# Putting a factor's high and low part side by side in products of 512 columns, in the up products of a blocked MLP

## The chip, the core and the metric

The kernel runs on one NeuronCore of a Trainium2 chip. The metric is the device time of one execution in microseconds (us), lower is better. TensorE (PE in the profile, with its weight loads listed as PEld), VectorE (DVE), ScalarE (ACT) and GpSimd (POOL) each work through an instruction stream of their own in order and wait for each other by semaphores; SyncE (SP) starts transfers.

## The reference

A decoder trunk of two layers on one sequence of 512 tokens of width 1024: layer 0 mixes by multi-head latent attention, layer 1 by sliding-window attention, and each is followed by a layer norm, the MLP below and another layer norm. The change lies in the two MLPs.

```python
def _mlp(x, w_up, w_down):            # x (1, 512, 1024), w_up (1024, 4096), w_down (4096, 1024)
    h = jax.nn.relu(x @ w_up)
    return (h * h) @ w_down

for l in range(DEPTH):                # DEPTH = 2
    ...
    x = _layernorm(alpha * x + y, ln_mix_g[l], ln_mix_b[l])
    x = _layernorm(alpha * x + _mlp(x, mlp_w_up[l], mlp_w_down[l]), ln_mlp_g[l], ln_mlp_b[l])
```

## The kernel before

**Precision.** Every float32 operand is split in two float32r parts, a high one (ACT copies it, in `split`, L78) and a low one (DVE subtracts, L86). A product takes three matmuls in place of one: high weight by high factor, high weight by low factor, low weight by high factor. `three` lists them.

**Seven products.** The hidden layer is cut in four blocks (`Block(q)`, q = 0 to 3) of 1024 hidden features. Within a block the up projection and the down projection are each computed as seven products of quarter matrices, in the manner of Strassen and Winograd: up products U1, U2, U5, U3, U6, U7, U4 and down products D1 to D7. M5 below is what U5 leaves, and so on. An up product (`Block.up`) has two weight tiles (i = 0, 1), two column halves of each (j = 0, 1) and four contraction steps (k = 0 to 3). For each of these 16 places it issues the three matmuls of 256 columns, 48 in all, and accumulates the two halves j of a tile i side by side in one PSUM bank of 512 columns: two banks a product. Behind the first block the three matmuls of a step follow each other. In the first block (q = 0) the order is by passes: first all of high by high, then high by low, then low by high, so that the low parts are wanted two passes later than the high ones. A down product (`Block.down_`) is 24 matmuls of 512 columns, 12 for each of two token tiles t, in one bank each.

**What becomes of the up products** (`up_out`). U1 and U2 accumulate into the same pair of banks: ACT copies M1 out to a scratch tile `u` when U1 is done (L756), U2 adds itself onto it in the bank, and ACT takes the sum through a relu (L758). M5 and M3 stay in their banks until U6 is done. Then DVE forms u += M6 (L764), v = M5 - u (L765) and a11 = M3 + v (L767), and from v and u later a21 and a22 (L770, L773). The first product that needs a bank again waits until its last reader is done.

**Order.** Tables of steps set the order of the products, of both kinds and of neighbouring blocks: a prime marks the later block.

```python
SECOND_STEPS = "U'1 U'2 D5 D3 U'5 D6 D7 U'3 D4 U'6 U'7 U'4 D'1 D'2"
STEPS = "U'1 D5 U'2 D3 U'5 D6 D7 U'3 D4 U'6 U'7 U'4 D'1 D'2"
FIRST_STEPS, LAST_STEPS = "U'1 U'2 U'5 U'3 U'6 U'7 D'2 U'4 D'1", "U'1 D5 U'2 D3 U'5 D6 D7 U'3 U'6 U'7 U'4 D4"
```

FIRST_STEPS run block 0, SECOND_STEPS the ups of block 1 among the downs of block 0, STEPS those of block 2, LAST_STEPS those of block 3. PE's program is in the order in which it is written (`pe`). What DVE and ACT do is put in order by the compiler's scheduler, and then executed in that order.

**Supply.** A ring of four weight tiles (each with its high part `wh` and low part `wl`) runs ahead of PE: DMA, ACT's split, DVE's split, use. PSUM has eight banks: six rotate under the tag "mm", two ("tr") serve transposes and U6. The scratch tiles of the MLP are called `uv`, the factors of the down products `fac`. The x factors, a combination of quarters of x for each n, are in tiles "xt" (`XFactors.part`): before, high and low parts are in separate tiles, `xth` and `xtl`, each of which holds two n. L573 and L576 add what a down product has left in its bank onto the residual x and so free that bank.

Of the kernel before, what the change touches and what calls it, by code (L numbers as in the profile page):

```python
# [10 lines left out]
F32R = mybir.dt.float32r  # L11
AF = mybir.ActivationFunctionType
# [4 lines left out]
P = 128  # L17
# [16 lines left out]
BANDW = 384  # L34
POOL_O, POOL_SO = (0, 2), (0, 1, 2, 3)
WARM = 18

ON_POOL = ("w_h", "w_o", "w_sq", "w_so")

# [11 lines left out]
def build(tc, nc, io, out):  # L51
    with ExitStack() as top:
        cp = top.enter_context(tc.tile_pool(name="cp", bufs=1))
        wp = top.enter_context(tc.tile_pool(name="wp", bufs=1))
        xp = top.enter_context(tc.tile_pool(name="xp", bufs=1))
# [7 lines left out]
        def nm(s):  # L63
            n_names[0] += 1
            return f"{s}_{n_names[0]}"
# [32 lines left out]
        def pe(ins):  # L98
            tc.keep_in_program_order(ins)
# [255 lines left out]
        b = bank()  # L355
# [3 lines left out]
        both = [xp.tile([P, 4, S], F32, tag="xt", bufs=8, name=nm("xw")) for _ in range(4)]  # L359
        both = [z.rearrange("p a b -> p (a b)") for z in both]  # L360
# [108 lines left out]
        class TokMajor:  # L469
# [15 lines left out]
            def part(self, t, kp):  # L485
                while len(self.w) <= kp:
                    self.w.append(weights(self.name))
                if t not in self.b:
                    self.b[t] = bank()
                self.group(self.b[t], t, kp, self.w[kp])  # L490
                self.done.add((t, kp))
                if kp == 3:
                    self.evac(t, slice(0, 512), self.b[t])
# [149 lines left out]
        class XFactors(Factors):  # L643


            def __init__(self, mp):
                super().__init__(mp)
                self.tiles = {}
                self.xf = [None] * 2

            def part(self, n, p):
                at = {1: (0, 0), 2: (0, 1), 5: (1, 0), 3: (1, 1), 6: (2, 0), 7: (2, 1), 4: (3, p)}[n]
                tile = (at[0], p if n != 4 else 0)
                if tile not in self.tiles:
                    self.tiles[tile] = xp.tile([P, 2, 4, 256], F32R, tag="xt", bufs=8, name=nm(("xth", "xtl")[p]))
                return self.tiles[tile][:, at[1]]
# [34 lines left out]
        def mlp(src, gb, dst, mp):  # L691
# [12 lines left out]
            own_bank = {1: 1, 2: 1, 5: 5, 7: 7, 4: 7, 6: 6}  # L704
# [4 lines left out]
            class Block:  # L709
# [13 lines left out]
                def quarter(self, name):  # L723
                    if name not in self.g:
                        self.g[name] = mp.tile([P, 4, 256], F32, tag=name, bufs=1, name=nm(name))
                    return self.g[name]

                def up(self, n):
                    w = [weights("up") for _ in range(2)]
                    key = {3: 3}.get(n) or own_bank[n]  # L730
                    for i in range(2):
                        b = self.bank(("U", key), i)
                        wh, wl = w[i]
                        steps = list(product(range(3), range(2), range(4)))
                        if self.q:
                            steps.sort(key=lambda step: step[1:])
                        for p, j, k in steps:
                            c = slice(j * 512 + k * P, j * 512 + (k + 1) * P)
                            group(
                                b[:, j * 256 : j * 256 + 256],  # L740
                                three(wh[:, c], wl[:, c], src.part(n, 0)[:, k, :], src.part(n, 1)[:, k, :])[p : p + 1],
                                n not in (2, 4) and (p, j, k) == (0, 0, 0), (p, k) == (2, 3), skip_group_check=True,
                            )
                        self.up_out(n, i)
                        if (self.q, i) == (0, 0) and n in (1, 2):
                            with tc.high_priority():
                                src.turn(n + 1)

                def up_out(self, n, i):
                    pairs = slice(2 * i, 2 * i + 2)  # L750
                    of = lambda key: self.banks[("U", key), i].rearrange("p (a b) -> p a b", a=2)
                    done = None
                    if n == 1:
                        if i == 0:
                            self.u = self.down.scratch()
                        nc.scalar.activation(self.u[:, pairs], of(1), AF.Copy)  # L756
                    elif n == 2:
                        nc.scalar.activation(self.quarter("a12")[:, pairs], of(1), AF.Relu)  # L758
                        if i == 1:
                            nc.scalar.activation(self.g["a12"], self.g["a12"], AF.Square)  # L760
                    elif n == 6:
                        if i == 0:
                            self.v = self.down.scratch()
                        nc.vector.tensor_add(self.u[:, pairs], of(6), self.u[:, pairs])  # L764
                        nc.vector.tensor_sub(self.v[:, pairs], of(5), self.u[:, pairs])  # L765
                        done = "a11"
                        nc.vector.tensor_add(self.quarter(done)[:, pairs], of(3), self.v[:, pairs])  # L767
                    elif n == 7:
                        done = "a21"
                        nc.vector.tensor_sub(self.quarter(done)[:, pairs], self.v[:, pairs], of(7))  # L770
                    elif n == 4:
                        done = "a22"
                        nc.vector.tensor_add(self.quarter(done)[:, pairs], of(7), self.u[:, pairs])  # L773
                    if done and i == 1:
                        nc.scalar.activation(self.g[done], self.g[done], AF.Relu)
                        nc.scalar.activation(self.g[done], self.g[done], AF.Square)
# [49 lines left out]
            at = {}  # L826
# [20 lines left out]
            b = blocks[NFF - 1]  # L847
# [5 lines left out]
            class Hidden:  # L853
# [6 lines left out]
                def of(self, p, k, cols):  # L860
                    n = ((2, 1), (4, 0))[cols.start // 256][k // 4]
                    return b.fac[n][:, p, k % 4, cols.start % 256 : cols.start % 256 + P]
# [12 lines left out]
        with tc.tile_pool(name="mla", bufs=1) as mp:  # L875
# [62 lines left out]
            for kp in range(4):  # L938
                wh, wl = weights("w_kv")
# [123 lines left out]
            w = weights("w_uv")  # L1063
# [427 lines left out]
```

## Time and profile before

| | |
|---|---|
| three timed runs | 997.42, 997.08, 996.26 us, median 997.08 |
| the profiled execution | 996.2 us |
| its span in the trace | 994.1 us, so 2.1 us lie around it |
| PE busy | 984.1 us, 99% of the span |
| DVE busy | 767.5 us, 77% |
| ACT busy | 554.5 us, 56% |
| POOL busy | 247.0 us, 25% |
| chain that ended last | PE 97%, of which matmuls of line L110 89% |

Read it as follows. An engine's busy time is the time in which at least one of its instructions was executing; matmuls overlap at their ends, so a single one appears longer than the distance to the next. The chain that ended last is followed back from the last instruction: each piece of it is work that something later had to wait for. Times inside the trace count from the span's start. The MLP of layer 0 runs from about 172 to 500 us, that of layer 1 from about 653 to 981 us.

### The profile page before, as it was taken

The numbers are of one execution on the slowest core, as the hardware profiler recorded it, in microseconds if no ns is written. First come the engines' busy times: TensorE is split into PE (matmuls) and PEld (weight loads), VectorE is DVE, ScalarE is ACT, GpSimd is POOL, SyncE is SP. The second block draws the span as 40 slices with busy tenths as digits, with TensorE's granted clock in tenths as the row PEclk, the third lists the DMA queues.
The fourth block names the chain that finished last, engine by engine and source line by source line (L and its number), as shares of the span: only waits on it lengthen the run. The fifth ranks groups of instructions, "written<-read, shape, count | busy, mean of one in ns | idle before, by whom it ended". The sixth has DMA issues, their size and how long they took to land.

```text
span 994.1 us, 15912 instructions
## 1 busy us (share of the span) xinstructions
PE 984.1 (99%) x6136; PEld 889.6 (89%) x6136; DVE 767.5 (77%) x1240; ACT 554.5 (56%) x847; POOL 247.0 (25%) x267
## 2 busy tenths in 40 slices
PE   9999999999999999999999999999999999999996
PEld 9888888999899999998899988889998998999986
DVE  6589857988878769786684678688995986888746
ACT  5557644457547547646156688546663663764710
POOL 1242101312212212210025675332131122022002
PEclk9999999999999999999999999999999999999999
DMA  7431125399789977963323211439798798798332
GB/s 262 135 98 43 64 106 191 105 214 235 147 186 234 173 170 218 227 107 129 104 78 103 86 65 54 170 64 240 215 184 190 181 201 177 167 261 142 79 127 84
DMA packets 60246, 149.55 MB, mean 150 GB/s; under 512 B 5211, under 2 KB 9740, under 8 KB 60172
## 3 DMA queue, kind: packets, MB, share of 16 engines
q0 software_dynamic: 24320, 58.73, 33.1%
q1 hardware_dynamic: 35564, 89.49, 26.4%
q8 instruction: 48, 0.79, 0.3%
q10 hardware_dynamic: 288, 0.33, 0.1%
q14 instruction: 26, 0.21, 0.1%
HBM read 146.41 MB, written 4.22 MB: 152 GB/s over the span
## 4 chain that ended last, share of the span: by engine, by line
PE 97%; DVE 1%; issue 0%; DMA 0%; ACT 0%; POOLq 0%; POOL 0%; DVEq 0%
PE mm L110 89%; PE tr L110 5%; PE tr L1130 1%; PE tr L1313 1%; PE tr L668 1%; PE tr L1315 1%; DMA xw<-in_xT 0%; PE tr L454 0%; PE mm L1054 0%; PE tr L908 0%; POOLq L1487 0%; POOL rs L416 0%; ACT p L1293 0%; DVE mm L1109 0%; DVE ql L86 0%
## 5 line engine op out<-in xcount | busy, mean ns | idle before, releaser
L110 PE MATMUL mm<-wh,fac 128*128 128x512 f32 (+1 forms) x944 | 283.5, 386 | 0.0
L78 ACT ACTIVATE wh<-wq 128x1024 fp32r<-128x1024 f32 x164 | 173.5, 1060 | 190.0 <-PE mm L110 134.9
L86 DVE TENSOR_TENSOR wl<-wq,wh 128x1024 fp32r<-128x1024 f32 x164 | 199.2, 1220 | 69.5 <-ACT wh L78 68.9
L110 PE MATMUL mm<-xth,wh 128*128 128x256 f32 (+1 forms) x936 | 222.1, 290 | 0.0
L110 PE MATMUL mm<-xth,wl 128*128 128x256 f32 (+1 forms) x808 | 210.5, 290 | 0.0
L110 PEld LDWEIGHTS mm<-wh,fac 128*128 128x128 f32 x944 | 175.6, 188 | 35.1 <-DVE fac L86 0.6
L110 PE MATMUL mm<-xtl,wh 128*128 128x256 f32 (+1 forms) x680 | 179.1, 292 | 0.0
L110 PE MATMUL mm<-wl,fac 128*128 128x512 f32 (+1 forms) x472 | 173.2, 386 | 0.0
L110 PEld LDWEIGHTS mm<-xth,wh 128*128 128x128 f32 x936 | 159.7, 192 | 3.0
L110 PEld LDWEIGHTS mm<-xth,wl 128*128 128x128 f32 x808 | 144.1, 192 | 2.3
L195 POOL DMA_DIRECT2D wq<-in_up x64 | 77.6, 1227 | 253.4 <-DVE wl L86 188.7
L78 ACT ACTIVATE wh<-raw 128x1024 fp32r<-128x1024 f32 (+2 forms) x81 | 81.9, 1015 | 81.5 <-PE mm L110 59.4
L110 PEld LDWEIGHTS mm<-xtl,wh 128*128 128x128 f32 x680 | 121.6, 192 | 2.8 <-DVE xtl L86 0.2
L110 PEld LDWEIGHTS mm<-wl,fac 128*128 128x128 f32 x472 | 88.8, 188 | 17.1
L86 DVE TENSOR_TENSOR wl<-raw,wh 128x1024 fp32r<-128x1024 f32 (+2 forms) x59 | 70.8, 1208 | 34.8 <-ACT wh L78 34.5
L195 POOL DMA_DIRECT2D wq<-in_down x48 | 42.0, 875 | 193.2 <-DVE wl L86 188.4
L416 POOL TENSOR_TENSOR rs<-v,half 128x1 f32<-128x1 f32 x24 | 28.7, 1196 | 190.5 <-DVE v L435 155.8
L84 POOL TENSOR_TENSOR wl<-raw,wh 128x256 fp32r<-128x256 f32 (+1 forms) x72 | 54.2, 786 | 65.7 <-ACT wh L78 62.4
L110 PE MATMUL mm<-wh,oh 128*128 128x512 f32 x128 | 50.9, 398 | 0.0
L110 PE MATMUL mm<-wh,ol 128*128 128x512 f32 x128 | 50.1, 391 | 0.0
L110 PE MATMUL mm<-wl,oh 128*128 128x512 f32 x128 | 49.9, 390 | 0.0
L576 DVE TENSOR_TENSOR x<-mm,x 128x512 f32<-128x512 f32 (+1 forms) x53 | 35.6, 674 | 14.5 <-PE mm L110 14.2
(229 smaller groups left out, 1776.1 us busy)
## 6 DMA issues: line engine op xcount, KB each, us to landing
wq<-in_up POOLq DMA_DIRECT2D x64, 512.0 KB, 7.9
wq<-in_down POOLq DMA_DIRECT2D x48, 512.0 KB, 7.1
wq<-in_up SPq DMA_DIRECT2D x32, 512.0 KB, 5.8
raw<-in_down SPq DMA_DIRECT2D x28, 512.0 KB, 6.4
wq<-in_down SPq DMA_DIRECT2D x24, 512.0 KB, 7.0
raw<-in_up SPq DMA_DIRECT2D x16, 512.0 KB, 4.1
raw<-in_w_o SPq DMA_DIRECT2D x8, 512.0 KB, 3.3
raw<-in_w_so SPq DMA_DIRECT2D x8, 512.0 KB, 3.5
```

Source lines behind the costliest of these rows:

```text
L78: high = nc.scalar.activation(dst_h, src, AF.Copy)
L84: low = engine.tensor_sub(dst_l[:, c : c + n], src[:, c : c + n], f32(dst_h[:, c : c + n]))
L86: low = (engine or nc.vector).tensor_sub(dst_l, src, f32(dst_h))
L110: pe(nc.tensor.matmul(dst, st, mv, start=first and i == 0, stop=last and i == len(pairs) - 1, **kw))
L195: nc.gpsimd.dma_start(half(a, jp), chunk(*more, jp), accum_op=ALU.add)
L416: nc.gpsimd.tensor_tensor(r, v, half, ALU.pow)
L576: nc.vector.tensor_add(xs[t][:, c], b, xs[t][:, c])
L668: pe(nc.tensor.transpose(pt[:, a, :], xs[t][:, k * P : (k + 1) * P], ident))
L1130: pe(nc.tensor.transpose(pt[:, kb * P : (kb + 1) * P], p[:, kb * P : (kb + 1) * P], ident))
L1313: pe(nc.tensor.transpose(pt[:, a, 0:P], p[:, kb, P:256], ident))
L1315: pe(nc.tensor.transpose(pt[:, a, P:256], p[:, kb + 1, 0:P], ident))
```

## The change

It issues some of the up products in another form, which the table `SIDE_BY_SIDE` names: U5 and U3 in every block, and U1 and U2 as well in blocks 1, 2 and 3. That is 2 + 3 x 4 = 14 products in a layer. At each of the 16 places, such a product has one matmul of 512 columns, whose moving operand is the factor's high and low part side by side (`both(n)[:, :, k, :]`, two pieces of 256 columns that lie 1024 elements apart) under the high weight, and one of 256 columns under the low weight. High by low so lands in the second half of the bank, and each (i, j) takes a bank of its own: four banks a product in place of two. The matmuls of a step follow each other, in block 0 too. A new helper, `side_out`, empties each bank as soon as its (i, j) is done: ACT copies the first half to SBUF and DVE adds the second half to that. M5 and M3 are then in SBUF (in `v` and `a11`) when U6 is done. For the x factors, one tile holds the two parts of one n (`PAIRED`, `xtb` in the program). In the sevenfold scheme nothing else is computed, and the DMAs, POOL's and SP's streams are unchanged. 448 matmuls (28 products x 16) fall away.

```diff
+SIDE_BY_SIDE = {0: (5, 3), 1: (1, 2, 5, 3), 2: (1, 2, 5, 3), 3: (1, 2, 5, 3)}
+PAIRED = (1, 2, 3, 4, 5, 6, 7)
...
+            def both(self, n):
+                if n not in self.tiles:
+                    self.tiles[n] = xp.tile([P, 2, 4, 256], F32R, tag="xt", bufs=8, name=nm("xtb"))
+                return self.tiles[n]
+
             def part(self, n, p):
+                if n in PAIRED:
+                    return self.both(n)[:, p]
...
+                def up_side(self, n, w):
+
+                    key = own_bank.get(n, n)
+                    for i, (wh, wl) in enumerate(w):
+                        for j in range(2):
+                            b = self.bank(("U", key), (i, j))
+                            for k in range(4):
+                                c = slice(j * 512 + k * P, j * 512 + (k + 1) * P)
+                                pe(nc.tensor.matmul(
+                                    b.rearrange("p (a b) -> p a b", a=2), wh[:, c], src.both(n)[:, :, k, :],
+                                    start=n not in (2, 4) and k == 0, stop=False, skip_group_check=True,
+                                ))
+                                pe(nc.tensor.matmul(
+                                    b[:, 0:256], wl[:, c], src.part(n, 0)[:, k, :],
+                                    start=False, stop=k == 3, skip_group_check=True,
+                                ))
+                            self.side_out(n, i, j, b)
...
+                def side_out(self, n, i, j, b):
...
+                    at = 2 * i + j
+                    one, two = b[:, 0:256], b[:, 256:512]
...
+                    else:
+                        to = {1: lambda: self.u, 2: lambda: self.quarter("a12"), 5: lambda: self.v,
+                              3: lambda: self.quarter("a11")}[n]()[:, at]
+                        nc.scalar.activation(to, one, AF.Copy)
+                        nc.vector.tensor_add(to, two, to)
+
                 def up(self, n):
                     w = [weights("up") for _ in range(2)]
+                    if self.side(n):
+                        return self.up_side(n, w)
...
                     elif n == 2:
-                        nc.scalar.activation(self.quarter("a12")[:, pairs], of(1), AF.Relu)
+                        if not self.side(2):
+                            nc.scalar.activation(self.quarter("a12")[:, pairs], of(1), AF.Relu)
+                        elif i == 1:
+                            nc.scalar.activation(self.g["a12"], self.g["a12"], AF.Relu)
...
-                        nc.vector.tensor_add(self.u[:, pairs], of(6), self.u[:, pairs])
-                        nc.vector.tensor_sub(self.v[:, pairs], of(5), self.u[:, pairs])
+                        if not self.side(6):
+                            nc.vector.tensor_add(self.u[:, pairs], of(6), self.u[:, pairs])
+                        m5 = self.v[:, pairs] if self.side(5) else of(5)
+                        nc.vector.tensor_sub(self.v[:, pairs], m5, self.u[:, pairs])
                         done = "a11"
-                        nc.vector.tensor_add(self.quarter(done)[:, pairs], of(3), self.v[:, pairs])
+                        m3 = self.quarter(done)[:, pairs] if self.side(3) else of(3)
+                        nc.vector.tensor_add(self.quarter(done)[:, pairs], m3, self.v[:, pairs])
```

Two places of the program show how the instructions stand. In the names, the number behind the last underscore tells buffers apart. PE first, in block 0 of layer 0: the second half of U'3 and the start of U'6 before, where `mm_459` and `mm_460` are M3's two banks.

```order
L110 MATMUL mm_459_2353<-xtl_437_2161,wh_447_2278 128x256 x8
L110 MATMUL mm_459_2353<-xth_436_2160,wl_448_2279 128x256 x8
L110 MATMUL mm_460_2378<-xth_436_2160,wh_449_2284 128x256 x8
L110 MATMUL mm_460_2378<-xtl_437_2161,wh_449_2284 128x256 x8
L110 MATMUL mm_460_2378<-xth_436_2160,wl_450_2285 128x256 x8
L110 MATMUL tr_466_2413<-xth_443_2240,wh_451_2289 128x256 x8
```

And now, the passage from U'3's second bank to its third, on PE:

```order
L749 MATMUL mm_464_2360<-xtb_438_2166,wh_447_2278 128x512
L753 MATMUL mm_464_2360<-xtb_438_2166,wl_448_2279 128x256
L749 MATMUL mm_464_2360<-xtb_438_2166,wh_447_2278 128x512
L753 MATMUL mm_464_2360<-xtb_438_2166,wl_448_2279 128x256
L749 MATMUL mm_465_2371<-xtb_438_2166,wh_449_2284 128x512
L753 MATMUL mm_465_2371<-xtb_438_2166,wl_450_2285 128x256
```

U'5 and U'3 together take eight banks (`mm_453`, `455`, `456`, `457`, then `462`, `464`, `465`, `466`) of the six that rotate. `mm_465` is the seventh and gets the bank of `mm_453`, the first (i, j) of U'5, so its first matmul has a semaphore wait for DVE's add that reads `mm_453`. Before, U'5 and U'3 had four banks and no such wait.

On DVE, the same stretch before (`wl_450` and `wl_452` are low weights for U'3 and U'6, `xth_445` and `xtl_444` x factors):

```order
L639 TENSOR_TENSOR uv_438_2164<-xf_406_1994,xf_432_2145 128x1024
L86 TENSOR_TENSOR wl_450_2285<-wq_446_2276,wh_449_2284 128x1024
L86 TENSOR_TENSOR fac_470_2473<-a12_440_2219,fac_470_2473 128x1024
L86 TENSOR_TENSOR wl_452_2290<-wq_393_1908,wh_451_2289 128x1024
L86 TENSOR_TENSOR xth_445_2247<-xf_432_2145,xth_445_2247 128x1024
```

And now:

```order
L642 TENSOR_TENSOR uv_437_2163<-xf_406_1994,xf_432_2145 128x1024
L89 TENSOR_TENSOR wl_450_2285<-wq_446_2276,wh_449_2284 128x1024
L89 TENSOR_TENSOR fac_474_2461<-a12_440_2219,fac_474_2461 128x1024
L89 TENSOR_TENSOR wl_452_2290<-wq_393_1908,wh_451_2289 128x1024
L787 TENSOR_TENSOR uv_454_2303<-mm_453_2294,uv_454_2303 128x256
L787 TENSOR_TENSOR uv_454_2303<-mm_455_2306,uv_454_2303 128x256
L787 TENSOR_TENSOR uv_454_2303<-mm_456_2317,uv_454_2303 128x256
L787 TENSOR_TENSOR uv_454_2303<-mm_457_2328,uv_454_2303 128x256
```

The four adds of M5 stand behind the same instructions in the same order as before; `wl_452` is the one right ahead of them.

The second place is DVE in block 1 of layer 0, around the two additions onto x that free D5's banks. Before:

```order
L573 SCALAR_TENSOR_TENSOR x_375_1820<-x_375_1820,mm_522_2841 128x512
L639 TENSOR_TENSOR uv_511_2762<-a11_468_2441,a21_477_2511 128x1024
L86 TENSOR_TENSOR fac_528_2905<-uv_509_2756,fac_528_2905 128x1024
L573 SCALAR_TENSOR_TENSOR x_376_1822<-x_376_1822,mm_523_2855 128x512
L86 TENSOR_TENSOR wl_521_2837<-wq_491_2593,wh_520_2836 128x1024
```

And now, from the low factor of D3 (`fac_516`) on, with the four adds of M2 (`a12_523`):

```order
L89 TENSOR_TENSOR fac_516_2740<-uv_517_2742,fac_516_2740 128x1024
L787 TENSOR_TENSOR a12_523_2766<-mm_509_2690,a12_523_2766 128x256
L787 TENSOR_TENSOR a12_523_2766<-mm_511_2702,a12_523_2766 128x256
L787 TENSOR_TENSOR a12_523_2766<-mm_512_2713,a12_523_2766 128x256
L787 TENSOR_TENSOR a12_523_2766<-mm_513_2724,a12_523_2766 128x256
L642 TENSOR_TENSOR uv_517_2742<-a11_463_2357,a21_481_2499 128x1024
L89 TENSOR_TENSOR fac_534_2876<-uv_515_2736,fac_534_2876 128x1024
L576 SCALAR_TENSOR_TENSOR x_376_1822<-x_376_1822,mm_529_2826 128x512
```

D3's second token tile accumulates in the bank from which `x_376` is added (D5 and D3 share their banks), so its first matmul waits for that addition. The four adds of M2 now stand ahead of it; those of M1, four more, stand earlier in the same program, among the weights.

## Rows read from the trace of the kernel before

**Rows 1.** The page: busy time of the engines, and the chain by engine.
```profile
PE 984.1 (99%) x6136; PEld 889.6 (89%) x6136; DVE 767.5 (77%) x1240; ACT 554.5 (56%) x847; POOL 247.0 (25%) x267
...
PE 97%; DVE 1%; issue 0%; DMA 0%; ACT 0%; POOLq 0%; POOL 0%; DVEq 0%
```

**Rows 2.** Waits of PE, first and last of five: total, times, longest.
```profile
PE mm L110 <- POOL zeros L354: 1.1, 1, 1.1
...
PE tr L1130 <- DVE ri L1117: 0.2, 1, 0.2
```

**Rows 3.** The chain in order of time: start, length, what, count.
```profile
172.00 5.46 PE mm L110 x24
...
194.16 14.39 PE mm L110 x120
208.55 5.76 PE tr L110 x48
...
438.75 5.76 PE tr L110 x48
```

**Rows 4.** PE's timeline at U'5 of block 0: start, length, instruction, count.
```profile
196.87 1.12 PE L110 MATMUL mm<-xth,wh 128*128 128x256 f32 x8
197.83 1.12 PE L110 MATMUL mm<-xtl,wh 128*128 128x256 f32 x8
...
677.97 1.12 PE L110 MATMUL mm<-xth,wh 128*128 128x256 f32 x8
```

**Rows 5.** DVE's timeline there, in both layers; in brackets the idle time before.
```profile
196.33 1.29 DVE L86 TENSOR_TENSOR xtl<-uv,xth 128x512 fp32r<-128x512 f32 x2
...
199.74 1.23 DVE L86 TENSOR_TENSOR wl<-wq,wh 128x1024 fp32r<-128x1024 f32 x1 [0.79 <-ACT wh L78]
...
206.03 1.22 DVE L86 TENSOR_TENSOR wl<-wq,wh 128x1024 fp32r<-128x1024 f32 x1
207.17 1.21 DVE L86 TENSOR_TENSOR xth<-xf,xth 128x1024 fp32r<-128x1024 f32 x1
...
688.26 1.21 DVE L86 TENSOR_TENSOR xth<-xf,xth 128x1024 fp32r<-128x1024 f32 x1
```

**Rows 6.** Windows: length, busy PE, PEld, DVE, ACT, POOL; granted clock, DMA.
```profile
200.00:205.00 5.00, 5.00 (x44) 5.00 (x43) 5.00 (x6) 3.43 (x5) 1.20 (x1) 1.00 1.08 295
205.00:210.00 5.00, 5.00 (x44) 5.00 (x43) 5.00 (x5) 3.66 (x4) 2.41 (x2) 1.00 1.13 211
210.00:215.00 5.00, 5.00 (x44) 5.00 (x44) 2.35 (x3) 2.62 (x3) 1.20 (x1) 1.00 1.13 207
```

**Rows 7.** Groups by shape: count, busy, mean ns of one, idle before.
```profile
L86 DVE TENSOR_TENSOR pt<-tr,pt 128x256 fp32r<-128x256 f32 x8 | 3.3, 417 | 0.9 <-ACT pt L78 0.9
...
L78 ACT ACTIVATE pt<-tr 128x256 fp32r<-128x256 f32 x8 | 3.1, 382 | 1.9 <-PE tr L1130 1.9
```

**Rows 8.** DVE's timeline at D5 and D3, block 1.
```profile
249.48 1.23 DVE L86 TENSOR_TENSOR wl<-wq,wh 128x1024 fp32r<-128x1024 f32 x1 [0.52 <-ACT wh L78]
...
254.63 0.68 DVE L573 SCALAR_TENSOR_TENSOR x<-x,mm 128x512 f32<-128x512 f32 x1
255.23 2.35 DVE L86 TENSOR_TENSOR wl<-wq,wh 128x1024 fp32r<-128x1024 f32 x2
```

**Rows 9.** PE's timeline at the start of D5, block 1.
```profile
248.26 0.63 PE L110 MATMUL mm<-wh,fac 128*128 128x512 f32 x2
```

**Rows 10.** Windows from U'1 to the end of U'3, blocks 1 to 3.
```profile
236.80:281.50 44.70, 44.70 (x289) 40.91 (x288) 36.31 (x36) 24.49 (x26) 10.19 (x11) 1.00 0.91 179
315.40:360.10 44.70, 44.70 (x289) 40.89 (x289) 32.90 (x33) 23.77 (x25) 10.05 (x10) 1.00 0.90 179
393.90:438.70 44.80, 44.80 (x289) 40.98 (x289) 37.47 (x40) 24.77 (x27) 12.45 (x12) 1.00 0.92 190
```

**Rows 11.** DVE's timeline ahead of U'6 of block 3.
```profile
433.82 1.22 DVE L86 TENSOR_TENSOR wl<-wq,wh 128x1024 fp32r<-128x1024 f32 x1
```

More of the change, by code (lines that the diff above doesn't have):

```diff
@@ L649, in __init__ @@
                 self.xf = [None] * 2
+            def both(self, n):
+                if n not in self.tiles:
+                    self.tiles[n] = xp.tile([P, 2, 4, 256], F32R, tag="xt", bufs=8, name=nm("xtb"))
+                return self.tiles[n]
             def part(self, n, p):
+                if n in PAIRED:
+                    return self.both(n)[:, p]
                 at = {1: (0, 0), 2: (0, 1), 5: (1, 0), 3: (1, 1), 6: (2, 0), 7: (2, 1), 4: (3, p)}[n]
-                tile = (at[0], p if n != 4 else 0)
+                tile = (at[0], p if n != 4 else 0, "")
                 if tile not in self.tiles:
@@ L726, in quarter, with side @@
                     return self.g[name]
+                def side(self, n):
+                    return n in SIDE_BY_SIDE[self.q]
+                def up_side(self, n, w):
[14 more added lines that the diff above has]
+                            self.side_out(n, i, j, b)
+                        if n in (2, 6, 7, 4):
+                            self.up_out(n, i)
+                        if (self.q, i) == (0, 0) and n in (1, 2):
+                            with tc.high_priority():
+                                src.turn(n + 1)
@@ new lines, in side_out @@
+                def side_out(self, n, i, j, b):
+                    if (n, i, j) == (1, 0, 0):
+                        self.u = self.down.scratch()
+                    if (n, i, j) == (5, 0, 0):
+                        self.v = self.down.scratch()
+                    at = 2 * i + j
+                    one, two = b[:, 0:256], b[:, 256:512]
+                    if n == 6:
+                        for part in (one, two):
+                            nc.vector.tensor_add(self.u[:, at], part, self.u[:, at])
+                    elif n == 7:
+                        to = self.quarter("a21")[:, at]
+                        nc.vector.tensor_sub(to, self.v[:, at], one)
+                        nc.vector.tensor_sub(to, to, two)
+                    elif n == 4:
+                        to = self.quarter("a22")[:, at]
+                        nc.vector.tensor_add(to, one, self.u[:, at])
+                        nc.vector.tensor_add(to, two, to)
[3 more added lines that the diff above has]
+                        nc.scalar.activation(to, one, AF.Copy)
+                        nc.vector.tensor_add(to, two, to)
@@ L761, in up_out @@
                     elif n == 6:
-                        if i == 0:
+                        if i == 0 and not self.side(5):
                             self.v = self.down.scratch()
-                        nc.vector.tensor_add(self.u[:, pairs], of(6), self.u[:, pairs])
-                        nc.vector.tensor_sub(self.v[:, pairs], of(5), self.u[:, pairs])
+                        if not self.side(6):
+                            nc.vector.tensor_add(self.u[:, pairs], of(6), self.u[:, pairs])
+                        m5 = self.v[:, pairs] if self.side(5) else of(5)
+                        nc.vector.tensor_sub(self.v[:, pairs], m5, self.u[:, pairs])
                         done = "a11"
-                        nc.vector.tensor_add(self.quarter(done)[:, pairs], of(3), self.v[:, pairs])
+                        m3 = self.quarter(done)[:, pairs] if self.side(3) else of(3)
+                        nc.vector.tensor_add(self.quarter(done)[:, pairs], m3, self.v[:, pairs])
                     elif n == 7:
                         done = "a21"
-                        nc.vector.tensor_sub(self.quarter(done)[:, pairs], self.v[:, pairs], of(7))
+                        if not self.side(7):
+                            nc.vector.tensor_sub(self.quarter(done)[:, pairs], self.v[:, pairs], of(7))
                     elif n == 4:
                         done = "a22"
-                        nc.vector.tensor_add(self.quarter(done)[:, pairs], of(7), self.u[:, pairs])
+                        if not self.side(4):
+                            nc.vector.tensor_add(self.quarter(done)[:, pairs], of(7), self.u[:, pairs])
                     if done and i == 1:
```

## The prediction

> **What bounds the kernel now.** I read the page first: PE is busy for 984.1 of 994.1 us and the chain is PE for 97% [rows 1]. Then PE's waits: five in the whole run, the longest 1.1 us at the start, the least 0.2 us [rows 2]. So the MLPs run at the pace at which PE issues matmuls, at a granted clock of 1.00 [rows 6, 10], its 2.4 GHz level. Two things follow. Whatever shortens PE's stream counts in full. And whatever PE newly waits for counts in full too, since no wait stands there that could hide it.
>
> The pace is in the chain [rows 3]: 48 matmuls of 256 columns take 5.76 us, 120 ns each; 24 of 512 columns take 5.46 us, 227.5 ns each. Two of 256 cost 240 ns, one of 512 costs 227.5: a matmul costs 12.5 ns besides its columns.
>
> **The change part by part.**
>
> *Fewer matmuls.* 28 products lose 16 matmuls each. 448 x 12.5 ns = 5.6 us less, 2.8 us a layer; a product falls from 5.76 to 5.56 us. The row is for whole operands. The new operand comes in two pieces, and no MLP row of before shows such a one; its bounds are 12.5 ns less and, from the other side, as much as the two matmuls that it replaces, a gain of nothing. A gain beyond 5.6 us I exclude, because the columns stay. I take 5.6, since each piece is a row of 256 elements like the operands measured. The Trainium skill, "TensorE: Matmul & The Clock Gate", section "Wait — 56ns, not 53.3ns?", gives about 2.5 ns as a matmul's fixed cost at the fast clock. By it the gain would be 448 x 2.5 ns = 1.1 us and my sum 4.5 us higher; the rows show 12.5 ns here, and I go by them.
>
> *The start of U'5 in block 0.* By passes, U'5 wanted the low part of its x factor 0.96 us after its start: 196.87 and 197.83 [rows 4]. Now the first matmul takes both parts. The low part's second half is the first of the two `xtl` that start at 196.33 in 1.29 us [rows 5], so it ends near 197.0. PE waits 0.15 us plus a handover; I take 0.25, bounds 0.15 and 0.35. Nothing hides it.
>
> *The bank in U'3 of block 0.* U'3's third (i, j) needs the bank of M5's first. The order of before shows what DVE does ahead of that add: it goes down to `wl_452`, the split at 206.03, and the next instruction starts at 207.17 [rows 5]. DVE is busy for 10.00 us of 200 to 210 [rows 6], so the add cannot come sooner unless that queue starts sooner. It starts at 207.17 and takes 0.42 (a 128x256 pass of DVE out of PSUM, 417 ns [rows 7]), so the bank is free at 207.59. PE gets there at 196.87 + 0.25 + U'5's 5.56 + half of U'3's, 2.78, = 205.46. It waits 2.13 us, with a handover 2.2. In layer 1 the instruction behind the split starts at 688.26 [rows 5] and U'5 at 677.97 [rows 4]: 688.68 - 686.56 = 2.12. Bounds 1.4 (if DVE's idle 0.79 us at 199.74 [rows 5] goes away) and 2.4. The three adds of M5 that follow find their banks done, so the fourth bank of U'3 is in time, and DVE, idle for 2.65 us of 210 to 215 [rows 6], catches up on the 1.7 us that four adds cost. Behind PE's wait everything on PE is shifted by as much; nothing gives it back.
>
> *D3 in block 1.* D3's second token tile needs the addition onto `x_376`, at 254.63 in 0.68, over at 255.31 [rows 8]. PE wants it 36 matmuls of 227.5 ns behind D5's start at 248.26 [rows 9], at 256.45: 1.14 us of margin. Two faster products ahead (U'1, U'2) take 0.40 of it: 0.74. M2's four adds now stand in front: 4 x 0.417 = 1.67 us. The wait is 0.93, I take 0.9. It is 0 if DVE has idle time left there (it has 0.52 us at 249.48 [rows 8]) and the adds, back to back, cost less; it is 8 x 0.417 - 0.74 = 2.6 if M1's four count in full too. The layers have the same program here, so twice.
>
> *What I cost at nothing.* U'2 accumulates in U'1's banks and so waits for M1's adds; it comes back to a bank 3 x 1.39 = 4.17 us after U'1 left it, while a copy (382 ns) and an add (417 ns [rows 7]) take 0.80. What covers it is 3.4 us for whatever stands ahead on DVE, two or three instructions of 1.2 us; uncovered it costs their rest, about 1 us. ACT gets four more copies a product, 4 x 0.382 = 1.5 us, less the passes of 512 that fall away at U1 and U2; it is at 23.8 to 24.8 of 44.7 us [rows 10]. In blocks 2 and 3 a down product lies between U'1 and U'2, and every bank comes back at least a product later than it was left. M5 and M3 read from SBUF instead of PSUM at U6: same count, same shapes. DMAs, POOL and SP have the same streams; POOL's weight DMAs wait for DVE's splits, and a split that is late moves them, which only the DVE case below would turn into time.
>
> **Sum.** A layer: -2.8 + 0.25 + 2.2 + 0.9 = +0.55; two: +1.1 us. Against the profiled 996.2 us (994.1 and 2.1 around it): 997.3. The median of the three runs, 997.08, lies 0.9 above that execution, so I forecast **998.2 us**. Its own range: with all waits low, -5.6 + 2 x (0.15 + 1.4 + 0) = -2.5, so 994.6; with all high, -5.6 + 2 x (0.35 + 2.4 + 2.6) = +5.1, so 1002.2. 0.2% of this kernel, about 2 us, is what a measurement of it can tell from no change.
>
> **The rivals.**
>
> *Faster: DVE comes earlier than its old order says.* DVE's dense stretch from 200 to 210 us starts after an idle 0.79 us, for which it waits for ACT [rows 5]. If ACT's new order brings that split earlier, U'3's wait is 1.4 in place of 2.2, and if DVE's idle in block 1 swallows the adds, D3's goes: 998.2 - 2 x 0.8 - 2 x 0.9 = 994.8. With none of the waits it would be 997.08 - 5.6 = 991.5. For it: DVE has idle 8.4 of 44.7 us in block 1's stretch [rows 10]. Against: that ACT's split there waits for the ring and PE's order ahead of it hasn't changed. Chance 0.22.
>
> *Slower: the operand in two pieces is dear.* If a matmul of 512 columns with a jump in the middle costs what two of 256 cost, the 5.6 us are gone and the waits stay: 998.2 + 5.6 = 1003.8. It decides from little: at 2 ns more for each of the 448, 0.9 us, the sum is 2.0 over before. For it: no row has such an operand. Against: a piece is 256 elements long, one jump in 512. The Trainium skill, "Advanced Engine Details and Errata", section "PSUM Cachelines", states that any non-contiguous access pattern slows matmuls significantly; no row here shows it, and if it held for this jump the gain would be the first thing to go. Chance 0.15, with the case that the change so does not do what it says.
>
> *Slower: DVE falls behind in blocks 1 and 3.* From U'1 to U'3 of block 3 it is busy 37.47 of 44.8 us [rows 10]. Sixteen adds of 0.417 make 44.1, while PE's 44.8 shrinks by 0.83 to 44.0. It is full, and what is idle before (7.3 us) is waits for ACT and PE that may not vanish: if all stay, DVE ends 44.1 + 7.3 - 44.0 = 7.4 us late. The weights' low parts are ahead of PE by some microseconds (433.82 + 1.22 = 435.04 against U'6 at 438.75, 3.7 us [rows 3, 11]), so 3.7 us are left as PE's wait, 7.4 in both layers: 1005.6. It decides from half of that idle on. For it: the load. Against: idle that is a wait for ACT shrinks when DVE comes late. Chance 0.13.
>
> **How the numbers follow.** The forecast case has 0.50: 0.38 within 0.2%, 0.10 slower (a D3 wait in its upper half), 0.02 faster. Rival one is faster, 0.22. Of the two slow rivals' 0.28 some 0.02 stay within 0.2%. So faster 0.24, same 0.40, slower 0.36. The range 992.5 to 1004.0 leaves out the waitless case below and most of the DVE case above, about 0.08 and 0.12.
>
> **What would show it.** Distances of PE in a new product: 347.5 ns for a pair of 512 and 256 columns, 5.56 us for sixteen; if it is 360, the second rival. In PE's waits: two of about 2.2 us for DVE (L787) near 205 and 687 us, two of 0.25 us at the start of U'5, two of about 0.9 us for L576 near 256 and 737. If the first are missing, my reading of DVE's order is wrong. If PE waits for `wl` of L89 in block 3, it is the third rival; DVE then shows hardly any idle time before 439 us.

## The result, and the profile after

The changed kernel takes 1001.26 us (median of five runs, 1000.41 to 1003.4), the kernel before 997.03 (five runs, 996.26 to 997.42): a ratio of 1.005, 95% interval 1.0039 to 1.006. It is slower by 4.2 us. The forecast was 998.2, within 0.2%, with a range of 992.5 to 1004.0: the range holds the time, the sign was given a chance of 0.36, the likeliest case was another.

The profiled execution of after took 1000.41 us with a span of 998.2, 4.1 us more than before. Its page and PE's waits answer to [rows 1, 2] (busy time, share, instructions; then line, waited for, total, times, longest):

```profile
PE 983.2 (98%) x5688; PEld 866.1 (87%) x5688; DVE 803.6 (81%) x1352; ACT 582.1 (58%) x941; POOL 247.1 (25%) x267
```

```profile
PE mm L749 <- DVE uv L787: 3.8, 2, 1.9
PE mm L113 <- DVE x L576: 1.3, 2, 0.7
PE mm L113 <- POOL zeros L357: 1.1, 1, 1.1
```

PE issues 448 matmuls fewer and is busy only 0.9 us less, and there are four new waits, two of 1.9 us and two of 0.7: M5's bank in U'3 of block 0, and the addition onto x at D3 of block 1, in each layer. They are the two places that the prediction named.

The first place, PE's timeline (start, length, instruction; in brackets the idle time before), against [rows 4]:

```profile
205.95 0.28 PE L753 MATMUL mm<-xtb,wl 128*128 128x256 f32 x1
208.14 0.47 PE L749 MATMUL mm<-xtb,wh 128*128 128x512 f32 x1 [1.91 <-DVE uv L787]
```

and DVE's there, against [rows 5]:

```profile
206.44 1.22 DVE L89 TENSOR_TENSOR wl<-wq,wh 128x1024 fp32r<-128x1024 f32 x1
207.58 1.41 DVE L787 TENSOR_TENSOR uv<-mm,uv 128x256 f32<-128x256 f32 x4
```

The four adds stand right behind the split, and the first is what PE waits for. The second place, DVE's timeline against [rows 8], and PE's:

```profile
253.46 0.69 DVE L576 SCALAR_TENSOR_TENSOR x<-x,mm 128x512 f32<-128x512 f32 x1
254.06 1.22 DVE L89 TENSOR_TENSOR fac<-uv,fac 128x1024 fp32r<-128x1024 f32 x1
255.20 1.41 DVE L787 TENSOR_TENSOR a<-mm,a 128x256 f32<-128x256 f32 x4
256.53 1.21 DVE L642 TENSOR_TENSOR uv<-a,a 128x1024 f32<-128x1024 f32 x1
...
258.80 0.68 DVE L576 SCALAR_TENSOR_TENSOR x<-x,mm 128x512 f32<-128x512 f32 x1
```

```profile
259.53 0.73 PE L113 MATMUL mm<-wh,fac 128*128 128x512 f32 x2 [0.67 <-DVE x L576]
```

M2's adds stand in front of the second addition, which ends at 259.48 (258.80 + 0.68), and the matmul starts at 259.53. (Idle time counts from the modelled end of the last matmul; by the starts of matmuls, below, the delay here is nearly 1 us.)

Since the weight tiles come in the same order in both programs, the start of the first matmul under each can be set against before. How late after is, in us (layer 0 and layer 1):

```
                                         layer 0         layer 1
into U'5 of block 0                       +0.21           +0.26
into the second half of U'3, block 0      +2.01           +1.95
behind D3, block 1                        +0.96           +0.98
over a side-by-side product elsewhere     -0.113          -0.113
```

Fourteen products at 0.113 us make 1.6 us a layer. Added up, the two layers give 2 x (0.23 + 1.98 + 0.97 - 1.58) = +3.2 of the 4.1 us between the two spans. Of the rest, 0.4 is there before the first MLP (the two executions start apart), 0.35 comes inside the two MLPs (0.1 of it at the first matmul of each U'5, the rest in smaller pieces), and 0.1 between them.

### The profile page after: what moved, and what is told of

The parts are those of the page before. It is cut to its first block, busy times and chain, and to the rows that moved or that the text cites. A ratio compares the mean times of both kernels' runs of the same rounds, so it can differ in the third digit from the quotient of the medians.

```text
span 998.2 us, 15247 instructions
## 1 busy us (share of the span) xinstructions
PE 983.2 (98%) x5688; PEld 866.1 (87%) x5688; DVE 803.6 (81%) x1352; ACT 582.1 (58%) x941; POOL 247.1 (25%) x267
## 5 line engine op out<-in xcount | busy, mean ns | idle before, releaser
L749 PE MATMUL mm<-xtb,wh 128*128 128x512 f32 x448 | 159.5, 399 | 3.9 <-DVE uv L787 3.8
L753 PE MATMUL mm<-xtb,wl 128*128 128x256 f32 x448 | 125.7, 281 | 0.0
L749 PEld LDWEIGHTS mm<-xtb,wh 128*128 128x128 f32 x448 | 84.2, 188 | 25.4 <-issue 4.3
L113 PE MATMUL mm<-xtb,wh 128*128 128x256 f32 x512 | 86.0, 283 | 0.0
L753 PEld LDWEIGHTS mm<-xtb,wl 128*128 128x128 f32 x448 | 84.6, 189 | 0.9
L113 PEld LDWEIGHTS mm<-xtb,wh 128*128 128x128 f32 x512 | 76.0, 192 | 0.2
L113 PE MATMUL mm<-xtb,wl 128*128 128x256 f32 x256 | 63.3, 283 | 0.0
```

Source lines behind the costliest of these rows:

```text
L113: pe(nc.tensor.matmul(dst, st, mv, start=first and i == 0, stop=last and i == len(pairs) - 1, **kw))
L749: pe(nc.tensor.matmul(b.rearrange("p (a b) -> p a b", a=2), wh[:, c], src.both(n)[:, :, k, :], start=n not in (2, 4) and k == 0, stop=Fals ...
L753: pe(nc.tensor.matmul(b[:, 0:256], wl[:, c], src.part(n, 0)[:, k, :], start=False, stop=k == 3, skip_group_check=True,))
```

## The experiments

Times are medians against the kernel before on the same chip, whose medians were 996.55 (first four), 996.64 (next four) and 996.21 us (next two); the two repeats at the end stand beside one execution of it at 997.23.

**Long and short matmuls in groups.** A pair of 512 and 256 columns took 353 ns in after, not 347.5. The first two runs ask why.

```diff
+                            for k in range(4):
+                                c = slice(j * 512 + k * P, j * 512 + (k + 1) * P)
                                 pe(nc.tensor.matmul(
                                     b[:, 0:256], wl[:, c], src.part(n, 0)[:, k, :],
```

> Of each (i, j) of a side-by-side product, the four matmuls of 512 columns come first and the four of 256 behind them; nothing else changes. In the changed kernel a pair of 512 and 256 columns takes 353 ns on PE, not the 347.5 of my sum. Theory A, the alternation of long and short matmuls costs the 6 ns: a pair here is 347.5 ns, a product 5.56 us instead of 5.65, 28 products give 2.5 us back: 998.7 us. Theory B, the operand's jump between its two pieces costs it: still 353 ns, 1001.3 us.

998.2 us, ratio 1.0017 (1.0008 to 1.0026). In PE's timeline of block 2, after (left of each line the start):

```profile
340.77 0.40 PE L749 MATMUL mm<-xtb,wh 128*128 128x512 f32 x1
...
341.83 0.40 PE L749 MATMUL mm<-xtb,wh 128*128 128x512 f32 x1
```

and in groups:

```profile
340.89 1.09 PE L749 MATMUL mm<-xtb,wh 128*128 128x512 f32 x4
341.82 0.63 PE L755 MATMUL mm<-xtb,wl 128*128 128x256 f32 x4
342.30 1.09 PE L749 MATMUL mm<-xtb,wh 128*128 128x512 f32 x4
```

Three pairs lie between the first two rows: 1.06 us, 353 ns a pair. Four pairs lie between the last two starts of long matmuls: 1.41 us, too coarse to tell 351 ns a pair from 353. By the starts under the weight tiles a product gains 0.147 us here, in place of 0.113: (5.76 - 0.147) / 16 makes 351 ns a pair, (5.76 - 0.113) / 16 makes 353. So the alternation costs about 2 of the 6 ns, not all: theory A holds for a third. The time fell by more than grouping can give (28 x 0.034 = 1.0 us): one of the two waits at D3, 1.0 us, is missing in this trace, its clock stays at 1.00 behind both waits in U'3, and most of the runs lie close together (nine of eleven from 997.79 to 998.99). How much each of these gives to the median is not shown.

**One piece in place of two.**

```diff
-                    self.tiles[n] = xp.tile([P, 2, 4, 256], F32R, tag="xt", bufs=8, name=nm("xtb"))
+                    self.tiles[n] = xp.tile([P, 4, 2, 256], F32R, tag="xt", bufs=8, name=nm("xtb"))
...
-                    return self.both(n)[:, p]
+                    return self.both(n)[:, :, p]
...
-                                    ..., wh[:, c], src.both(n)[:, :, k, :],
+                                    ..., wh[:, c], src.both(n)[:, k],
```

> The x factor's tile is laid out so that for each k the high and the low part follow each other without a jump (the moving operand of 512 columns is one piece); long and short matmuls alternate as in the changed kernel. Theory B, the jump costs the 6 ns a pair: 347.5 ns, 998.7 us. Theory A, the alternation costs it: 353 ns a pair as before, 1001.3 us.

1001.54 us, ratio 1.005 (1.0038 to 1.0063): no difference from after. PE's timeline at the same place:

```profile
340.96 0.40 PE L749 MATMUL mm<-xtb,wh 128*128 128x512 f32 x1
...
342.02 0.40 PE L749 MATMUL mm<-xtb,wh 128*128 128x512 f32 x1
```

Three pairs in 1.06 us again. From a long matmul to the next short one it is 236 ns on average in both kernels. The jump costs nothing, at least among alternating matmuls; theory B falls. In groups, long follows long at 232 ns, against 227.5 in the down products [rows 3]. What these last 4 ns are was not tried (one piece and groups together).

**Block 0 without it.**

```diff
-SIDE_BY_SIDE = {0: (5, 3), ...
+SIDE_BY_SIDE = {0: (), ...
```

> Block 0 has no side-by-side product (24 remain). Theory, the wait for the bank in U'3 of block 0 (2.0 us a layer by the profile) and for the low part at U'5 (0.2) are lost time that nothing gives back: less 2 x 2.2 us, and the products' own small gain goes with them: 996.9 us. Rival, PE's delay there has let DVE and the weights catch up, and without it the wait at D3 of block 1 or one for weights grows by as much: 999 us or more.

997.8 us, ratio 1.001 (1.0001 to 1.0019). PE's waits:

```profile
PE mm L113 <- DVE x L576: 1.4, 2, 0.7
PE mm L113 <- POOL zeros L357: 1.1, 1, 1.1
PE mm L113 <- ACT p L1364: 0.9, 1, 0.9
```

The waits for L787 are gone, D3's are what they were, not grown: the theory's case. The time is 0.9 us over its number. 0.45 of that is the gain of the four products themselves (4 x 0.113), which the expectation names and leaves out of its sum; and the trace has a new wait in the attention of layer 1, the last row, of which more below.

**Block 1 without U1 and U2.**

```diff
-SIDE_BY_SIDE = {..., 1: (1, 2, 5, 3), ...
+SIDE_BY_SIDE = {..., 1: (5, 3), ...
```

> In block 1 only U5 and U3 are side by side; U1 and U2 are as before. Theory, M1's and M2's eight adds on DVE are what makes D3 wait for the addition onto x (0.96 us a layer): that wait goes, two products a layer lose their gain of 0.11 us each: 1001.3 - 2 x (0.96 - 0.22) = 999.8 us. Rival, D3's wait comes from DVE's lag behind block 0: it stays, and the time is 1001.3 + 0.45 = 1001.7 us.

1000.91 us, ratio 1.0044 (1.0032 to 1.0057). PE's waits, all that are longer than 0.3 us:

```profile
PE mm L749 <- DVE uv L787: 3.8, 2, 1.9
PE mm L113 <- POOL zeros L357: 1.1, 1, 1.1
PE mm L113 <- ACT p L1364: 1.0, 1, 1.0
PE mm L113 <- ACT xth L81: 0.5, 1, 0.5
```

No wait for L576 is left, so M1's and M2's adds were D3's wait, as the theory says; but the time is 1.1 us over the theory's and hardly moved. The trace has two new waits in and behind the attention of layer 1 (1.0 and 0.5 us), which are as large as the gain; that they stand in the other executions too is not shown. In this execution, at 1002.7 us the slowest of the five, the clock also fell behind both waits in U'3 (below).

**M5's first banks elsewhere.**

```diff
-                            b = self.bank(("U", key), (i, j))
+                            b = self.banks["U", key, i, j] = tbank() if (self.q, n, i) == (0, 5, 0) else self.bank(("U", key), (i, j))
```

> In block 0 the first two of U'5's four banks are taken from the two of the tag tr, which are idle there, instead of the six of the tag mm; U'3 then finds its banks free, and the adds of M5 stand where they stood. Theory, the bank alone makes PE wait in U'3: both waits of 1.9 us go, and with them what the clock loses behind them in some executions (the median of the changed kernel, 1001.3, lies 0.9 above its profiled execution, in which the clock stayed at 1.00): 996.4 to 997.3 us. Rival, DVE's backlog is the cause and only the place changes: U'6, which needs the tr banks again, waits instead, and the time stays above 1000 us.

1004.01 us, ratio 1.0076 (1.0063 to 1.009): slower than after. PE's waits, and its timeline behind U'4 of block 0:

```profile
PE mm L113 <- ACT fac L81: 4.1, 2, 2.0
PE mm L113 <- DVE x L576: 1.3, 2, 0.7
```

```profile
233.12 0.73 PE L113 MATMUL mm<-wh,fac 128*128 128x512 f32 x2 [2.03 <-ACT fac L81]
```

The bank theory was right about the bank: no wait in U'3, none in U'6. But a wait as long stands 25 us later, for the factor of D'1 of block 0. ACT makes it at 232.03, behind a weight split:

```profile
231.08 1.04 ACT L81 ACTIVATE wh<-wq 128x1024 fp32r<-128x1024 f32 x1
232.03 1.04 ACT L81 ACTIVATE fac<-a 128x1024 fp32r<-128x1024 f32 x1
```

In after it stands at 229.67, and ACT has 41 weight splits of the program ahead of it; here there are 43. With the banks moved, the compiler's scheduler has put ACT's and DVE's instructions of this stretch in another order. Behind the new wait the clock falls too, in both layers of this trace (0.59 from 234 to 236 us). The time is the rival's, above 1000 us, but U'6, which it named, does not wait: neither rival holds as I put it, and the wait moves by way of the order.

**M2 emptied behind the additions onto x.**

```diff
-                            self.side_out(n, i, j, b)
+                            if (self.q, n) == (1, 2):
+                                self.late.append((i, j, b))
+                            else:
+                                self.side_out(n, i, j, b)
...
+                def late_out(self, freed):
+                    with behind((freed,)):
+                        for i, j, b in self.late:
+                            self.side_out(2, i, j, b)
...
                     blocks[q].down_(n)
+                    if (q, n) == (0, 5):
+                        blocks[1].late_out(blocks[0].freed)
```

Here `freed` is D5's last addition onto x, and `behind` orders what it encloses after it.

> In block 1 M2's four banks are emptied behind the additions onto x of D5 instead of ahead of the second one. Theory, the four adds of M2 in front of that addition are D3's wait (0.96 us a layer, in the profile as 0.7 of PE idle): it goes, 1001.3 - 1.9 = 999.3 us. Rival, they only move: U'5 of block 1 or its weights wait for what is now late, and the time stays at 1001 us.

999.04 us, ratio 1.0025 (1.0016 to 1.0033). DVE's timeline at the place, and PE's waits:

```profile
257.35 1.22 DVE L89 TENSOR_TENSOR fac<-uv,fac 128x1024 fp32r<-128x1024 f32 x1
258.48 0.68 DVE L576 SCALAR_TENSOR_TENSOR x<-x,mm 128x512 f32<-128x512 f32 x1
259.08 1.41 DVE L800 TENSOR_TENSOR a<-mm,a 128x256 f32<-128x256 f32 x4
```

```profile
PE mm L752 <- DVE uv L800: 3.8, 2, 1.9
PE mm L113 <- POOL zeros L357: 1.1, 1, 1.1
```

The adds now follow the addition, D3's wait is gone in both layers, and nothing waits in its place. The theory's 999.3 is met. The profiled execution, at 999.34 us, has a fall of the clock behind U'3's wait in layer 0.

**The three mends together, and with the low weight first.** The first is grouped, M5's banks and M2 behind in one kernel; the second in addition swaps the two groups of four in U'5 of block 0.

> The changed kernel with three mends together: long and short matmuls in groups of four, M5's first two banks from the tag tr, M2 emptied behind the additions onto x. If the three costs are independent: 1001.3 less 2.6 (grouping, 28 x 0.09), 4.0 (U'3), 1.9 (D3) and 0.9 (clock) = 991.9 us, 5 us under the kernel before. If DVE, which is nearly full in blocks 1 and 3, becomes the bound once PE is faster, 994 us or more, with waits of PE for low weights.

> As the kernel with the three mends, and in block 0 U'5 issues the four matmuls under the low weight first, which need only the high part of the factor: the wait at U'5's start (0.2 us a layer) is covered by 0.48 us of matmuls. 0.4 us less than that kernel, 991.5 us, if that wait is the low part's; no difference otherwise.

1000.55 us, ratio 1.0042 (1.003 to 1.0055), and 1000.56, ratio 1.0035 (1.0022 to 1.0048). Both traces have the same 4.1 us of waits for D'1's factor as the kernel with M5's banks moved, and no wait at D3 and none for low weights in blocks 1 to 3: DVE is not the bound there. Behind the wait for the factor the clock falls too, in both layers of the first trace and in layer 0 of the second. So the sum of independent mends failed at one of them, and both times lie some 9 us over what was expected. In the second, U'5's wait for the low part (0.30 us in the first) is gone, which the medians don't show under waits of 2 us and what follows them.

**Block 0 left alone, the rest mended.** Grouped, M2 behind, and no side-by-side product in block 0; then the same with U5 of block 0 as well.

```diff
-SIDE_BY_SIDE = {0: (5, 3), ...
+SIDE_BY_SIDE = {0: (), ...
```

In the second kernel the entry is `0: (5,)`.

> Block 0 as in the kernel before; in blocks 1 to 3 the side-by-side products, with long and short matmuls in groups of four; M2 of block 1 emptied behind the additions onto x. If the terms that the earlier runs showed are independent: 24 products at 0.208 us make 5.0 us, and no wait is left: 991.7 us against the kernel before at 996.64. Summed the other way, from the kernel without side-by-side products in block 0 (997.8), less 2 x 0.96 (D3) and 24 x 0.095 (grouping): 993.6 us. If DVE's load in blocks 1 and 3 makes PE wait once it is faster, 995 us or more.

> As the kernel with block 0 untouched, but U5 of block 0 side by side too: with U'3 it then needs six banks, so the wait in U'3 does not come back. Two products more gain 0.42 us, two waits for the low part of its factor cost 0.4: the same time within 0.2 us. If the four adds of M5 alone make D'1's factor late in block 0, as the eight adds did with M5 in the tr banks, some 2 us more a layer: 996 us.

The first takes 994.61 us, 0.9983 (0.9974 to 0.9992) of the kernel before: faster than both kernels. PE's busy time and its waits:

```profile
PE 980.9 (99%) x5752; PEld 868.9 (88%) x5752; DVE 797.7 (80%) x1336; ACT 575.5 (58%) x925; POOL 247.0 (25%) x267
```

```profile
PE mm L113 <- POOL zeros L357: 1.1, 1, 1.1
PE mm L113 <- ACT p L1381: 0.7, 1, 0.7
```

No MLP has a wait left. It is 1.6 us faster, not 5: 24 products at 0.147 make 3.5, of which in this trace 0.9 and 0.4 us are lost in layer 1's attention and behind it (below); 0.6 us between the two stay open. The second takes 999.73, ratio 1.0043 (1.0029 to 1.0056). Its waits are for D'1's factor again, 3.6 us in all, and DVE's timeline shows how:

```profile
231.63 0.69 DVE L859 TENSOR_TENSOR a<-mm,uv 128x512 f32<-128x512 f32 x1 [1.05 <-PE mm L113]
232.24 1.21 DVE L89 TENSOR_TENSOR wl<-wq,wh 128x1024 fp32r<-128x1024 f32 x1
233.37 1.22 DVE L89 TENSOR_TENSOR fac<-a,fac 128x1024 fp32r<-128x1024 f32 x1
```

The factor's low part stands behind an addition that itself waits for PE's U'4, idle time of DVE and all; in the kernel before and in after it stands ahead of it. Behind these waits the clock falls as well, in layer 0. The second theory has the place right and the length nearly (2 us a layer); its 996 us were reckoned from the 991.7 that the kernel beside it missed by 2.9, and leave out the clock. U5 of block 0, with its four copies on ACT and four adds on DVE, was enough to change the order; which of them made the scheduler choose it was not tried.

**The changed kernel again.** Two more executions, for their traces.

> The changed kernel once more, for its trace. Its profiled execution (1000.41 us) lies 0.85 under the median of its runs, and the clock stayed at 1.00 behind both waits of 1.9 us. Theory, in its slower executions the granted clock falls behind one or both of these waits, as it did in four other kernels that keep them or their like, at 1.2 to 1.5 us each: 1001.3 us or more with a stretch near 0.50 behind a wait, 1000.4 without one.

> As the run beside it: 1001.3 us or more if the trace has a stretch of clock near 0.50 behind a wait in U'3 of block 0, 1000.4 us if it has none; 1002.7 or more with two.

1003.62 and 1001.42 us. Windows of the first behind its two waits (length; busy PE, PEld, DVE, ACT, POOL; granted clock, DMA share, GB/s):

```profile
205.00:208.00 3.00, 1.25 (x8) 0.83 (x6) 3.00 (x4) 3.00 (x7) 1.20 (x1) 1.00 1.14 231
208.00:209.00 1.00, 0.70 (x3) 0.69 (x4) 1.00 (x4) 1.00 (x3) 0.88 (x1) 0.81 1.09 201
209.00:212.00 3.00, 3.00 (x11) 2.52 (x10) 3.00 (x5) 2.37 (x5) 0.32 (x1) 0.50 1.13 206
212.00:214.00 2.00, 2.00 (x16) 1.92 (x16) 2.00 (x3) 0.71 (x2) 0.82 (x1) 0.99 1.12 206
...
691.00:693.00 2.00, 0.31 (x2) 0.30 (x3) 2.00 (x5) 2.00 (x4) 0.92 (x2) 1.00 1.14 209
693.00:695.00 2.00, 2.00 (x9) 1.74 (x8) 2.00 (x4) 1.14 (x2) 0.70 (x1) 0.58 1.12 204
695.00:697.00 2.00, 2.00 (x9) 1.67 (x8) 2.00 (x3) 1.33 (x2) 0.00 (x0) 0.57 1.14 212
```

and of the execution of after shown above, at the same place:

```profile
208.00:210.00 2.00, 1.86 (x11) 1.67 (x12) 2.00 (x4) 1.94 (x4) 1.16 (x1) 1.00 1.12 204
210.00:212.00 2.00, 2.00 (x16) 1.87 (x16) 2.00 (x4) 1.33 (x2) 0.00 (x0) 1.00 1.14 208
```

In the first, PE has stood idle for 2.05 us (in layer 1 1.84), starts again, and the granted clock is 0.50 (1.2 GHz) for some 3 us, behind both waits; the matmuls there lose some 1.5 us each time, beside the wait itself. In the second execution (1001.42) it falls behind the wait of layer 1 alone, which costs 1.5; in the profiled execution of after, at 1000.41, behind neither. No fall, one, two: 1000.4, 1001.4, 1003.6 us. The steps of 1.0 and 2.2 us differ because the executions also start apart: by the starts of matmuls they are 0.42, -0.06 and 0.58 us behind the kernel before ahead of the first MLP. Without that the steps are 1.5 and 1.6. The theory's bounds for one and two falls are met; neither new execution was without a fall, so its 1000.4 is still the execution that it was made from.

## Why the prediction was right and wrong

- **What bounds the kernel**: right. PE's four new waits and its shorter products, set against each other, are 3.2 of the 4.1 us between the two spans.
- **The bank in U'3**: right, with its cause. 2.2 us forecast, 1.9 of idle time and 2.0 of delay measured; DVE's queue stood as the order said.
- **D3 of block 1**: right in the place and in M2's adds, since moving them removed it; the size, 0.9 forecast against 0.96 and 0.98 measured, is in part luck. The four adds take 1.33 us (255.20 to 256.53, above), not 1.67, and U'1 and U'2 give 0.22, not 0.40. What made up for it was left out: D3's low factor stood ahead of the first of the two additions onto x,

```profile
250.63 1.22 DVE L86 TENSOR_TENSOR fac<-uv,fac 128x1024 fp32r<-128x1024 f32 x1
251.76 0.68 DVE L573 SCALAR_TENSOR_TENSOR x<-x,mm 128x512 f32<-128x512 f32 x1
```

  and now stands between the two (254.06, above), which is 1.14 us more, while the first addition follows PE closer by 0.5. The second addition so comes 4.17 us later than before (258.80 against 254.63 [rows 8]), PE 2.25: less the margin of 1.14, that makes 0.8 us.
- **The start of U'5**: 0.25 forecast, 0.21 and 0.26 measured.
- **Fewer matmuls**: the term that was mis-sized. 5.6 us forecast, 28 x 0.113 = 3.2 measured. I took the fixed 12.5 ns from streams of equal matmuls. In a stream that mixes 512 and 256 columns a pair takes 353 ns where the sum of the two rows is 347.5. The bounds held it (0 to 12.5 ns, measured 7), and I took an end instead of the middle. The estimate from the Trainium skill's 2.5 ns ("TensorE: Matmul & The Clock Gate", section "Wait — 56ns, not 53.3ns?") was 1.1 us; the measured gain lies between the two.
- **The rival of the two-piece operand**: its price came in part (2.4 of the 5.6 us), its mechanism did not. One piece in place of two changes nothing (236 ns from a long matmul to the next short one in both). The prediction took the Trainium skill's sentence on non-contiguous patterns ("Advanced Engine Details and Errata", section "PSUM Cachelines") for a warning about this operand; its section is on PSUM, while this operand lies in SBUF and has one jump in 512 columns, so the runs neither bear the sentence out for PSUM nor contradict it.
- **The rival of an earlier DVE**: did not happen. Both waits came, and DVE's queue at U'3 reached the adds at 207.58, where the old order gave 207.17 and this execution runs 0.42 late.
- **The rival of DVE in blocks 1 and 3**: did not happen. From U'1 to U'3 of block 3 it is busy 42.21 of 44.6 us, where [rows 10] had 37.47 of 44.8 and I had summed 44.1; adds that follow each other take 1.41 us for four, not 1.67, and no weight was late:

```profile
396.20:440.80 44.60, 44.60 (x227) 37.78 (x227) 42.21 (x55) 28.20 (x39) 12.46 (x12) 1.00 0.92 195
```

- **What was left out**: "Behind PE's wait everything on PE is shifted by as much; nothing gives it back." It costs more than its length. Behind a wait of 1.9 us the granted clock fell in some executions, and then PE lost 1.5 us more. The prediction priced a new wait by its length alone, and read a clock of 1.00 from a kernel that had no such wait behind its first microseconds [rows 2].

With these two corrected, my own sum would have been -3.2 + 2 x (0.25 + 2.2 + 0.9) = +3.5, and each fall of the clock 1.5 more. Measured are +4.1 between the two spans without a fall, 0.4 of it from ahead of the first MLP, and +4.2 between the medians. The slower side would have been the forecast.

## What to carry to other kernels

Where the bounding engine has no waits, price a new wait by its length and by what the clock may do behind it, and look for it in the order of the engine that frees the buffer, as the static program gave the place of both waits here, and the length of the one in U'3 to 0.3 us. List everything that has changed its place in that order, not only the new instructions. Price an instruction from a stream of the same mix, not from streams of its own kind. Where a scheduler chooses the order of several engines, moving a buffer can reorder a stretch elsewhere, so a mend has to be read from its own trace.

## What the runs showed of the hardware

- After PE stood idle for 1.8 to 2.1 us in the middle of dense work, the granted clock fell to 0.50 for some 3 us in some executions and stayed at 1.00 in others of the same program: behind none, one or both of the two waits. Each fall behind U'3's wait cost about 1.5 us. With U5 alone side by side in block 0 it fell in layer 0 behind two waits of 0.7 and 1.2 us that end 2.4 us apart, and not in layer 1 behind two as long. Behind D3's wait of 0.7 us it fell in none of the traces.
- Matmuls of 512 and 256 columns that alternate take 236 and 117 ns from start to start, 353 a pair; in groups of four, 351; streams of one kind, 227.5 and 120 [rows 3]. A jump in the middle of the 512 columns makes no difference (236 ns with and without).
- In the one trace of each of three kernels (block 0 left out, with and without the mends, and block 1 without U1 and U2) one transfer issue of SP in layer 1's attention takes 1.4 to 2.0 us instead of 0.41, its data comes later, and PE loses 0.9 to 1.2 us there and 0.3 to 0.4 at the start of the next MLP. In the fastest kernel:

```profile
576.67 1.49 SPq L150 DMA_DIRECT2D raw<-in_w_so  x1
```

  and in the kernel before:

```profile
579.02 0.41 SPq L147 DMA_DIRECT2D raw<-in_w_so  x1
```

  It copies the same tensor in all kernels; why it takes longer in these three, and whether that goes with the kernel or with the execution, stays open.
